# A two-layer hybrid attention trunk: the next pair's attention values projected beside a pair's first head, and head outputs read out of PSUM behind their products

## The chip, the cores and the metric

The kernel runs on one core of a Trainium2 chip. The metric is the time of one execution in microseconds on the device, the median of three runs; a profile of one further execution gives the trace that is read here. PE is the matrix engine (its weight loads are listed apart as PEld), DVE the vector engine, ACT the scalar engine, POOL the GpSimd engine, SP the engine that issues most transfers.

## The reference

A trunk of two layers over 256 latent tokens `x` and 256 context tokens `ctx`, 1024 wide. In each layer a token mixer with three branches is followed by a feed-forward network with a convolution over three tokens:

- differential attention, 8 heads: two softmaxes per head, `w = p0 - lam * p1`, the head's output `w @ v`, then a root-mean-square norm over the 128 features of the head with a learned gain and a factor `1 - lam_init`;
- a chunked gMLP;
- a bidirectional HGRN2 recurrence, 8 heads, whose output gets a root-mean-square norm with a gain (`hg_norm_g`) and a product with `silu(g)`.

```
y_att = rmsnorm(o_att, att_subln_g) * (1 - lam_init)
y_hg  = rmsnorm(o_f + flip(o_b), hg_norm_g) * silu(g)
```

In the first layer the queries are all 512 tokens (`NQ = 512`), in the second only the 256 latent ones (`NQ = 256`); keys, values and the recurrence run over all 512 in both. The result is the latent stream.

## The kernel before

All activations stand transposed (features on the partitions) in the tile `X`, as a high and a low part in float32r; each product of two float32 numbers is made of three matmuls (`mm3`, lines 120 to 123). `load_w` (line 115) fetches a weight block of 512 KB in two parts of 128x1024: a transfer on SP (line 110), a cast to the high part on ACT (line 111), and the subtraction that gives the low part on DVE (line 112).

The stage of the change is the loop over the eight heads, lines 936 to 1003, once per layer. For each head `project` makes what the head needs: the gates, queries and output gates of the recurrence (`hg_proj`, line 367: 4 feature-major projections, `fm_steps`), queries and keys of the attention with their rotation (`att_proj`, line 568: 2 feature-major projections), and for every even head the values of a pair of heads, for the recurrence (`w_hi`) at the start and for the attention (`w_av`) at the end (`v_proj`, line 398, by `tm_steps`). `v_proj` gives one tile of 128 x 4 x 256 for both heads of a pair, copied out of PSUM by ACT (line 405); three such tiles exist.

A head's own work is two generators, the side work: `hg_head` (line 408; 13 steps between its yields) and `att_head` (line 588; 11 steps in the first layer, 7 in the second). The order in which PE gets its instructions is the order in which the program is written (`manual_schedule` for PE, line 1208); for the other engines a scheduler of the compiler orders what is ready. `weave` (line 821) writes PE's order: it runs `project(h + 1)` step by step and puts the side steps of head `h` between them, evenly over 0.92 of the steps that `units(h + 1)` announces: 12 for an odd head to be projected and 20 for an even one in the first layer, 9 and 17 in the second. So the side work of an even head lies beside the projection of an odd one, and the other way round. Head 7 is woven with `tail_proj` instead.

```
todo = sorted((((i + 1) / (c + 1) * n * rate, k) for k, c in enumerate(counts) for i in range(c)))
```

At the end of a head `rms_square` (line 314) squares the output `o` out of its PSUM bank on ACT (line 316), casts the squares (line 192, ACT) and subtracts (line 193, DVE); a step of `weave` later `rms_scale` (line 323) sums them over the partitions with two matmuls into another bank (line 321) and makes the reciprocal root on ACT (lines 327, 328). Then DVE reads `o` a second time: line 550 in `hg_head`, followed by the product with the gate of line 551, and line 644 in `att_head`. `put` stores the result to DRAM through SP.

PSUM has two pools of four banks: `pm` for the projections, `ps` for the heads (scores, levels, turned weights, `o`, column sums).

Of the kernel before, what the change touches and what calls it, by code (L numbers as in the profile page):

```python
# [13 lines left out]
AF = mybir.ActivationFunctionType  # L14
# [3 lines left out]
P = 128  # L18
# [3 lines left out]
HEADS = 8  # L22
# [25 lines left out]
def trunk(ctx: ExitStack, tc: tile.TileContext, A, out):  # L48
    nc = tc.nc
    sub, mul, add, amin, amax = ALU.subtract, ALU.mult, ALU.add, ALU.min, ALU.max  # L50
# [9 lines left out]
    @contextmanager  # L60
    def pool(name, side="left", **tags):
        with tc.tile_pool(name=name, bufs=1, side=side, reuse_waits="tile") as p:
            def get(tag, shape, dt=F32):
                return p.tile(shape, dt, tag=tag, name=tag, bufs=tags[tag])
            yield get
# [34 lines left out]
    def pk(l, n):  # L100
        a, b = PK[n]
        return pack[l][:, a:b]
# [211 lines left out]
    def rms_square(get, o, n):  # L314
        sq = get("sq", [P, 512])
        nc.scalar.activation(out=sq[:, :n], in_=o, func=AF.Square)
        return sq, split(get("sqs", [P, 2, n], F32R), sq[:, :n])
# [80 lines left out]
    def v_proj(get, src, X, out, name, w=None):  # L398
        if w is None:
            w = load_w(src)  # L400
        v = get("v", [P, 4, 256])
        for tt in range(2):
            ps = PB([P, 2, 256])
            yield from tm_steps(w, X, (2 * tt, 2 * tt + 1), ps)
            nc.scalar.copy(out=v[:, 2 * tt:2 * tt + 2, :], in_=ps)
        out[name] = v

    def hg_head(get, l, h, z, k, q, gg, v, put, lbv, C0, NQ):
# [3 lines left out]
        if l > 0:  # L412
            s = get("E", [P, 2, NT])
            nc.scalar.activation(out=s, in_=z, func=AF.Exp)
            for d in range(2):
                nc.vector.tensor_scalar(out=s[:, d, :], in0=s[:, d, :], scalar1=lbv[:, 1, d, h:h + 1], scalar2=2.0 ** -60,
                                        op0=mul, op1=amax)
# [13 lines left out]
        sc = get("sc", [P, NS, 2, T])  # L431
# [108 lines left out]
        for s in range(NS):  # L540
# [3 lines left out]
            if s == 0:  # L544
                for d in range(2):
                    nc.tensor.matmul(o[:, c], lhsT=st[:, d, :], rhs=V[:, d, 0:T], start=False, stop=(d == 1))  # L546
        sq = rms_square(get, o, NQ)
        yield
        r = rms_scale(sq, NQ)
        nc.vector.scalar_tensor_tensor(out=r[:, :NQ], in0=o, scalar=pk(l, "hgn"), in1=r[:, :NQ], op0=mul, op1=mul)  # L550
        nc.vector.tensor_tensor(out=r[:, :NQ], in0=r[:, :NQ], in1=gg, op=mul)
        put(r[:, :NQ])

# [34 lines left out]
    def att_head(get, l, qk, v, put, av, NQ):  # L588
        sc = 64 ** -0.5
        o = None  # L590
# [39 lines left out]
        for i in range(n + 2):  # L630
# [7 lines left out]
            if 1 <= i <= n:  # L638
                ws[i - 1] = turn(*ps.pop(i - 1))
                yield  # L640
        sq = rms_square(get, o, NQ)
        yield
        r = rms_scale(sq, NQ)
        nc.vector.scalar_tensor_tensor(out=r[:, :NQ], in0=o, scalar=av[:, 1:2], in1=r[:, :NQ], op0=mul, op1=mul)
        put(r[:, :NQ])
        yield

# [288 lines left out]
    for l in range(DEPTH):  # L936
# [5 lines left out]
        def putter(b, h):  # L942
            return lambda t: nc.sync.dma_start(out=ysp[b, h], in_=t)
# [20 lines left out]
        whi = load_w(A["w_hi"][l, 0])  # L964
        pre = nc.scalar.preload_act_table_set("natural_log_exp_and_others")
        tc.keep_in_program_order(pre)
        with pool("heads", lk=2, qg=1, qk=1, v=3, w=2, sq=2, sqs=2 if l else 1, wt=2, sc=1, E=6 if l else 4, K=2, p=2) as get, ExitStack() as even, \
                tc.issue_after(pre.ins):
            gete = even.enter_context(pool("even", lk=2, qg=1, qk=1, t=3, sh=2))
            gets = [lambda tag, *a: (gete if tag in ("lk", "qg", "qk", "t", "sh") else get)(tag, *a),  # L970
                    lambda tag, *a: (gete if tag in ("t", "sh") else get)(tag, *a)]

            def project(h, out, pss=None):
                if pss is not None:
                    yield from hg_proj(gets[h % 2], l, h, Xh, NQ, out, pss)
                if h % 2 == 0:
                    yield from v_proj(get, A["w_hi"][l, h // 2], Xh, out, "vh", whi if h == 0 else None)
                if pss is None:
                    yield from hg_proj(gets[h % 2], l, h, Xh, NQ, out)
                yield from att_proj(gets[h % 2], l, h, Xh, rope, NQ, out)  # L980
                if h % 2 == 0:
                    yield from v_proj(get, A["w_av"][l, h // 2], Xh, out, "va")

            def units(h):
                return (12 if l == 0 else 9) + (8 if h % 2 == 0 else 0)

            d = {}
            for _ in project(0, d, first):
                pass
            for h in range(HEADS):  # L990
                j = slice((h % 2) * P, (h % 2 + 1) * P)
                m = [hg_head(get, l, h, d["ls"], d["k"], d["qg"][:, 0, :], d["qg"][:, 1, :], d["vh"][:, :, j], putter(1, h),
                             lbv, (reset, masks), NQ),
                     att_head(get, l, d["qk"], d["va"][:, :, j], putter(0, h), attv[l], NQ)]
                if h + 1 < HEADS:
                    main, n = project(h + 1, d), units(h + 1)
                else:
                    even.close()
                    getv = rvt.enter_context(pool("vt", side="right", vt=ns))
                    vt = [getv("vt", [P, D]) for _ in range(ns)]  # L1000
                    pus = []
                    main, n = tail_proj(l, Xh, vt, ns, NQ, pus), 8 * ns // 2 + ns
                weave(main, n, m, (13, 2 * ns + 3), 0.92 if h + 1 < HEADS else (0.7, 0.85)[l])
# [208 lines left out]
```

## Time and profile before

| what | value |
|---|---|
| median of 3 runs | 2232.55 us (2230.82 to 2233.64) |
| the profiled execution | 2240.42 us |
| its span, first to last instruction | 2238.6 us |
| mean granted clock of PE | 0.981 of full speed |
| instructions | 32836 |
| moved by DMA | 293.21 MB |

The profile is of one execution. Busy times of PE have modelled ends: two matmuls that follow each other overlap in it, so the distance of their starts is what one takes. A wait is put down to the engine and line that came last before it. Line numbers are those of the kernel before.

### The profile page before, as it was taken

The numbers are of one execution on the slowest core, as the hardware profiler recorded it, in microseconds if no ns is written. First come the engines' busy times: TensorE is split into PE (matmuls) and PEld (weight loads), VectorE is DVE, ScalarE is ACT, GpSimd is POOL, SyncE is SP. The second block draws the span as 40 slices with busy tenths as digits, with TensorE's granted clock in tenths as the row PEclk, the third lists the DMA queues.
The fourth block names the chain that finished last, engine by engine and source line by source line (L and its number), as shares of the span: only waits on it lengthen the run. The fifth ranks groups of instructions, "written<-read, shape, count | busy, mean of one in ns | idle before, by whom it ended". The sixth has DMA issues, their size and how long they took to land. (4 is left out here: it accounts for less than half of the span.)

```text
span 2238.6 us, 32836 instructions
## 1 busy us (share of the span) xinstructions
PE 2136.9 (95%) x12448; PEld 1860.9 (83%) x12448; DVE 1713.4 (77%) x2869; ACT 1155.8 (52%) x1920; POOL 315.7 (14%) x272
## 2 busy tenths in 40 slices
PE   8999999999999998989999998999999989997998
PEld 7888788887888886878887877988888879997997
DVE  6799888989767884358776766898899976567786
ACT  3766665656543223245342334666666655455664
POOL 3332132322200000011000002222221210001000
PEclk9999999999999999999999999999999999998999
DMA  7212212212255754344555653322222336654554
GB/s 283 94 67 73 70 66 76 73 65 66 62 174 193 235 161 112 94 159 136 166 187 182 198 148 105 104 91 90 81 90 86 97 99 218 195 183 142 186 194 138
DMA packets 93488, 293.21 MB, mean 131 GB/s; under 512 B 16017, under 2 KB 20753, under 8 KB 93073
## 3 DMA queue, kind: packets, MB, share of 16 engines
q1 hardware_dynamic: 93042, 290.59, 40.1%
q8 instruction: 98, 1.61, 0.3%
q14 instruction: 60, 0.49, 0.1%
q10 hardware_dynamic: 288, 0.52, 0.1%
HBM read 282.66 MB, written 8.41 MB: 130 GB/s over the span
## 5 line engine op out<-in xcount | busy, mean ns | idle before, releaser
L121 PE MATMUL pm<-X,wh 128*128 128x512 f32 (+1 forms) x2032 | 716.1, 352 | 11.0 <-DVE X L255 6.5
L122 PE MATMUL pm<-X,wh 128*128 128x512 f32 (+1 forms) x2032 | 699.0, 344 | 0.0
L123 PE MATMUL pm<-X,wl 128*128 128x512 f32 (+1 forms) x2032 | 698.8, 344 | 0.0
L112 DVE TENSOR_TENSOR wl<-wr,wh 128x1024 fp32r<-128x1024 f32 (+1 forms) x402 | 496.8, 1242 | 203.5 <-ACT wh L111 198.9
L111 ACT CAST wh<-wr 128x1024 fp32r<-128x1024 f32 x408 | 422.0, 1039 | 310.7 <-PE pm L122 172.2
L121 PEld LDWEIGHTS pm<-X,wh 128*128 128x128 f32 x2032 | 386.8, 190 | 61.2 <-DVE X L255 7.9
L123 PEld LDWEIGHTS pm<-X,wl 128*128 128x128 f32 x2032 | 387.1, 190 | 47.3
L122 PEld LDWEIGHTS pm<-X,wh 128*128 128x128 f32 x2032 | 386.5, 190 | 42.1
L225 DVE SCALAR_TENSOR_TENSOR wj<-wa,scr 128x1024 f32<-128x1024 f32 x128 | 156.4, 1222 | 63.4 <-DMA wa<-in_ada_row 60.4
L447 POOL TENSOR_TENSOR K<-qg,E 128x512 f32<-128x512 f32 (+1 forms) x96 | 132.3, 1380 | 461.9 <-PE ps L507 304.3
L121 PE MATMUL pm<-wl,X 128*128 128x256 f32 (+1 forms) x608 | 188.0, 309 | 0.0
L122 PE MATMUL pm<-wh,X 128*128 128x256 f32 (+1 forms) x608 | 183.7, 302 | 0.0
L123 PE MATMUL pm<-wh,X 128*128 128x256 f32 (+1 forms) x608 | 183.7, 302 | 0.0
L202 POOL TENSOR_TENSOR s<-s,mhalf 128x1 f32<-128x1 f32 x26 | 14.3, 550 | 1078.4 <-DVE s L199 1052.7
L121 PE MATMUL pm<-ys,wh 128*128 128x512 f32 (+1 forms) x384 | 129.9, 338 | 10.6 <-ACT wh L111 7.4
L441 DVE TENSOR_TENSOR E<-lk 128x512 f32<-128x512 f32 (+1 forms) x192 | 124.4, 681 | 9.5 <-PE ps L546 8.1
L123 PE MATMUL pm<-ys,wl 128*128 128x512 f32 (+1 forms) x384 | 129.5, 337 | 0.0
L122 PE MATMUL pm<-ys,wh 128*128 128x512 f32 (+1 forms) x384 | 129.5, 337 | 0.0
L121 PEld LDWEIGHTS pm<-wl,X 128*128 128x128 f32 x608 | 117.7, 194 | 6.5 <-issue 2.2
L122 PEld LDWEIGHTS pm<-wh,X 128*128 128x128 f32 x608 | 117.8, 194 | 4.0
L123 PEld LDWEIGHTS pm<-wh,X 128*128 128x128 f32 x608 | 117.4, 193 | 4.2
L442 ACT ACTIVATE E<-E 128x1024 f32<-128x1024 f32 (+1 forms) x96 | 80.9, 846 | 59.9 <-DVE E L441 58.9
(250 smaller groups left out, 3541.3 us busy)
## 6 DMA issues: line engine op xcount, KB each, us to landing
wr<-in_w_up SPq DMA_DIRECT2D x88, 512.0 KB, 4.4
wa<-in_ada_row SPq DMA_DIRECT2D x80, 512.0 KB, 4.1
wr<-in_w_gate SPq DMA_DIRECT2D x48, 512.0 KB, 4.0
wr<-in_w_dn SPq DMA_DIRECT2D x40, 512.0 KB, 4.1
wr<-in_w_hqg SPq DMA_DIRECT2D x32, 512.0 KB, 3.6
wr<-in_w_hff SPq DMA_DIRECT2D x32, 512.0 KB, 3.6
wr<-in_w_aqk SPq DMA_DIRECT2D x32, 512.0 KB, 3.6
wr<-in_w_hi SPq DMA_DIRECT2D x16, 512.0 KB, 4.0
```

The costliest lines, as they stand in the source:

```text
L111: nc.scalar.copy(out=hi, in_=raw)
L112: eng.tensor_tensor(out=lo, in0=raw, in1=hi.bitcast(F32), op=sub)
L121: nc.tensor.matmul(ps, lhsT=lh, rhs=rl, start=first, stop=False)
L122: nc.tensor.matmul(ps, lhsT=lh, rhs=rh, start=False, stop=False)
L123: nc.tensor.matmul(ps, lhsT=ll, rhs=rh, start=False, stop=last)
L202: nc.gpsimd.tensor_tensor(out=r, in0=r, in1=mhalf, op=ALU.pow)
L225: nc.vector.scalar_tensor_tensor(out=junk, in0=raw, scalar=1.0, in1=scr[:, v, :], op0=mul, op1=mul, accum_out=mod[l][:, m, v:v + 1])
L441: nc.vector.tensor_tensor(out=dst, in0=ref if first else src, in1=src if first else ref, op=sub)
L442: nc.scalar.activation(out=E, in_=E, func=AF.Exp)
L447: nc.gpsimd.tensor_tensor(out=mkap(KQ[:], dims, NQ), in0=mkap(q, dims), in1=mkap(E[:], [[2 * b, np_], [b - NQ, 2], [1, b]], NQ), op=mul)
```

## The change

`v_proj` now gives a list of two tiles of 128 x 4 x 128, one per head of a pair, out of six such tiles, and copies each half out of PSUM by itself. The attention values of the first pair are projected with head 0 as before; those of pair `c` (1 to 3) at the end of `project` of the odd head 2c - 1, which is woven with the side work of the even head 2c - 2. The recurrence's values stay at the start of the even head. `units` says 16 for heads 1 to 6 in the first layer (13 in the second) and 12 (9) for head 7.

In `hg_head` DVE multiplies `o`, its gain and the gate into the gate's tile `gg` right behind `rms_square`, before the yield; behind `rms_scale` one product is left. In `att_head` ACT copies `o` with its gain into a new tile `u` of the tag `wt` at the same place, and DVE's operation behind `rms_scale` multiplies two tiles in SBUF.

```diff
--- before.py
+++ after.py
@@ -398,11 +398,12 @@
     def v_proj(get, src, X, out, name, w=None):
         if w is None:
             w = load_w(src)
-        v = get("v", [P, 4, 256])
+        v = [get("v", [P, 4, P]) for _ in range(2)]
         for tt in range(2):
             ps = PB([P, 2, 256])
             yield from tm_steps(w, X, (2 * tt, 2 * tt + 1), ps)
-            nc.scalar.copy(out=v[:, 2 * tt:2 * tt + 2, :], in_=ps)
+            for i in range(2):
+                nc.scalar.copy(out=v[i][:, 2 * tt:2 * tt + 2, :], in_=ps[:, :, i * P:(i + 1) * P])
         out[name] = v
 
     def hg_head(get, l, h, z, k, q, gg, v, put, lbv, C0, NQ):
@@ -545,9 +546,9 @@
                 for d in range(2):
                     nc.tensor.matmul(o[:, c], lhsT=st[:, d, :], rhs=V[:, d, 0:T], start=False, stop=(d == 1))
         sq = rms_square(get, o, NQ)
+        nc.vector.scalar_tensor_tensor(out=gg, in0=o, scalar=pk(l, "hgn"), in1=gg, op0=mul, op1=mul)
         yield
         r = rms_scale(sq, NQ)
-        nc.vector.scalar_tensor_tensor(out=r[:, :NQ], in0=o, scalar=pk(l, "hgn"), in1=r[:, :NQ], op0=mul, op1=mul)
         nc.vector.tensor_tensor(out=r[:, :NQ], in0=r[:, :NQ], in1=gg, op=mul)
         put(r[:, :NQ])
 
@@ -639,9 +640,11 @@
                 ws[i - 1] = turn(*ps.pop(i - 1))
                 yield
         sq = rms_square(get, o, NQ)
+        u = get("wt", [P, NQ])
+        nc.scalar.activation(out=u, in_=o, func=AF.Copy, scale=av[:, 1:2])
         yield
         r = rms_scale(sq, NQ)
-        nc.vector.scalar_tensor_tensor(out=r[:, :NQ], in0=o, scalar=av[:, 1:2], in1=r[:, :NQ], op0=mul, op1=mul)
+        nc.vector.tensor_tensor(out=r[:, :NQ], in0=r[:, :NQ], in1=u, op=mul)
         put(r[:, :NQ])
         yield
 
@@ -964,34 +967,36 @@
         whi = load_w(A["w_hi"][l, 0])
         pre = nc.scalar.preload_act_table_set("natural_log_exp_and_others")
         tc.keep_in_program_order(pre)
-        with pool("heads", lk=2, qg=1, qk=1, v=3, w=2, sq=2, sqs=2 if l else 1, wt=2, sc=1, E=6 if l else 4, K=2, p=2) as get, ExitStack() as even, \
+        with pool("heads", lk=2, qg=1, qk=1, v=6, w=2, sq=2, sqs=2 if l else 1, wt=2, sc=1, E=6 if l else 4, K=2, p=2) as get, ExitStack() as even, \
                 tc.issue_after(pre.ins):
             gete = even.enter_context(pool("even", lk=2, qg=1, qk=1, t=3, sh=2))
             gets = [lambda tag, *a: (gete if tag in ("lk", "qg", "qk", "t", "sh") else get)(tag, *a),
                     lambda tag, *a: (gete if tag in ("t", "sh") else get)(tag, *a)]
 
             def project(h, out, pss=None):
+
                 if pss is not None:
                     yield from hg_proj(gets[h % 2], l, h, Xh, NQ, out, pss)
                 if h % 2 == 0:
-                    yield from v_proj(get, A["w_hi"][l, h // 2], Xh, out, "vh", whi if h == 0 else None)
+                    yield from v_proj(get, A["w_hi"][l, h // 2], Xh, out, ("vh", h // 2), whi if h == 0 else None)
                 if pss is None:
                     yield from hg_proj(gets[h % 2], l, h, Xh, NQ, out)
                 yield from att_proj(gets[h % 2], l, h, Xh, rope, NQ, out)
-                if h % 2 == 0:
-                    yield from v_proj(get, A["w_av"][l, h // 2], Xh, out, "va")
+                c = 0 if h == 0 else (h + 1) // 2 if h % 2 and h < HEADS - 1 else None
+                if c is not None:
+                    yield from v_proj(get, A["w_av"][l, c], Xh, out, ("va", c))
 
             def units(h):
-                return (12 if l == 0 else 9) + (8 if h % 2 == 0 else 0)
+                return (12 if l == 0 else 9) + (4 if h < HEADS - 1 else 0)
 
             d = {}
             for _ in project(0, d, first):
                 pass
             for h in range(HEADS):
-                j = slice((h % 2) * P, (h % 2 + 1) * P)
-                m = [hg_head(get, l, h, d["ls"], d["k"], d["qg"][:, 0, :], d["qg"][:, 1, :], d["vh"][:, :, j], putter(1, h),
+                vh, va = d["vh", h // 2][h % 2], d["va", h // 2][h % 2]
+                m = [hg_head(get, l, h, d["ls"], d["k"], d["qg"][:, 0, :], d["qg"][:, 1, :], vh, putter(1, h),
                              lbv, (reset, masks), NQ),
-                     att_head(get, l, d["qk"], d["va"][:, :, j], putter(0, h), attv[l], NQ)]
+                     att_head(get, l, d["qk"], va, putter(0, h), attv[l], NQ)]
                 if h + 1 < HEADS:
                     main, n = project(h + 1, d), units(h + 1)
                 else:
```

## Rows read from the trace of the kernel before

**Rows 1.** The page, part 1: busy time, share of the span, instructions.

```profile
PE 2136.9 (95%) x12448; PEld 1860.9 (83%) x12448; DVE 1713.4 (77%) x2869; ACT 1155.8 (52%) x1920; POOL 315.7 (14%) x272
```

**Rows 2.** Waits of PE, 64 to 640 us: waiter, releaser, total us, times, longest.

```profile
PE ps L321 <- DVE sqs L193: 6.6, 6, 1.8
PE ps L626 <- DVE sc L465: 4.6, 3, 1.5
```

**Rows 3.** Waits of PE, 1415 to 1850 us.

```profile
PE ps L321 <- DVE sqs L193: 10.3, 7, 2.7
PE ps L619 <- DVE p L613: 3.2, 1, 3.2
```

**Rows 4.** Busy time by stretch, layer 0: units beside head 1, head 2, the pair.

```profile
core 0: us, PE busy (x) PEld busy (x) DVE busy (x) ACT busy (x) POOL busy (x), PEclk, DMA share, GB/s
...
171.26:217.95 46.69, 46.35 (x259) 39.29 (x258) 44.58 (x77) 28.06 (x50) 13.96 (x9) 1.00 0.20 68
...
232.60:293.25 60.65, 55.32 (x294) 45.25 (x292) 57.01 (x98) 38.37 (x68) 17.37 (x10) 0.97 0.20 70
156.34:293.25 136.91, 131.24 (x778) 112.54 (x776) 118.38 (x204) 83.31 (x146) 38.45 (x26) 0.99 0.21 70
```

**Rows 5.** The same, layer 1: beside head 3, head 4, the pair, the slow clock.

```profile
1606.67:1638.12 31.45, 31.45 (x202) 28.16 (x201) 26.53 (x47) 19.43 (x37) 4.54 (x6) 1.00 0.31 101
...
1653.58:1695.10 41.52, 38.00 (x239) 32.27 (x238) 39.01 (x77) 27.46 (x54) 8.56 (x9) 0.99 0.29 96
1590.14:1695.10 104.96, 100.55 (x666) 89.71 (x666) 93.70 (x187) 67.46 (x130) 22.37 (x24) 0.97 0.26 86
1589.60:1595.30 5.70, 5.70 (x27) 5.70 (x28) 5.70 (x15) 3.24 (x7) 1.41 (x2) 0.50 0.15 42
```

**Rows 6.** PE in order of time: start us, us, line, [idle before <- releaser].

```profile
1586.26 0.40 PE L122 MATMUL pm<-X,wh 128*128 128x512 f32 x1
1586.49 0.39 PE L123 MATMUL pm<-X,wl 128*128 128x512 f32 x1
1589.57 0.77 PE L321 MATMUL ps<-sqs,onesr 128*128 128x256 f32 x2 [2.69 <-DVE sqs L193]
...
1595.79 0.28 PE L121 MATMUL pm<-wl,X 128*128 128x256 f32 x1
1595.91 0.28 PE L122 MATMUL pm<-wh,X 128*128 128x256 f32 x1
```

**Rows 7.** DVE by line, pair of layer 0: xcount | busy us, mean ns.

```profile
L112 DVE TENSOR_TENSOR wl<-wr,wh 128x1024 fp32r<-128x1024 f32 x16 | 20.9, 1309 | 4.5 <-ACT wh L111 4.5
...
L361 DVE SCALAR_TENSOR_TENSOR t<-pm,t 128x512 f32<-128x512 f32 x4 | 2.7, 683 | 0.4 <-ACT t L356 0.4
...
L374 DVE SCALAR_TENSOR_TENSOR lk<-pm,t 128x512 f32<-128x512 f32 x4 | 2.7, 678 | 0.0
...
L577 DVE STREAM_SHUFFLE sh<-pm 128x256 f32<-128x256 f32 x4 | 1.8, 445 | 0.0
...
L550 DVE SCALAR_TENSOR_TENSOR sq<-ps,pack,sq 128x512 f32<-128x512 f32 x2 | 1.5, 744 | 0.0
...
L551 DVE TENSOR_TENSOR sq<-sq,qg 128x512 f32<-128x512 f32 x2 | 1.4, 690 | 0.0
```

**Rows 8.** DVE by line, pair of layer 1.

```profile
L361 DVE SCALAR_TENSOR_TENSOR t<-pm,t 128x256 f32<-128x256 f32 x4 | 1.7, 416 | 0.1
...
L550 DVE SCALAR_TENSOR_TENSOR sq<-ps,pack,sq 128x256 f32<-128x256 f32 x2 | 1.0, 476 | 0.0
```

**Rows 9.** ACT by line, pair of layer 0.

```profile
L316 ACT ACTIVATE sq<-ps 128x512 f32<-128x512 f32 x4 | 2.4, 596 | 3.2 <-PE ps L543 3.2
L405 ACT COPY v<-pm 128x512 f32<-128x512 f32 x4 | 2.3, 580 | 2.7 <-PE pm L123 2.7
...
L621 ACT COPY wt<-ps 128x256 f32<-128x256 f32 x4 | 1.4, 359 | 0.1
```

## The prediction

> **What bounds the kernel now.** I read the page's busy shares first: PE is busy 95% of the span and DVE 77% [rows 1]. The stages with `project` and the heads (64 to 640 us and 1415 to 1850 us) are where the diff acts, so next I asked for PE's waits there. The longest are the column sums of line 321, which wait for DVE's split of line 193: 6.6 us in layer 0 and 10.3 us in layer 1 [rows 2, 3]. PE runs in the written order, so whatever DVE delivers late stops the projections queued behind it too.
>
> Then I cut one pair of heads at the boundaries of the projections. Call a unit the stretch between two yields of `project`. A feature-major unit is 12 matmuls of 512 columns, 0.23 us apart, 2.76 us; a value unit is 24 of 256 columns, 0.12 us apart, 2.88 us [rows 6]. While an odd head's side work runs, PE has 20 units to weave it into in layer 0 (17 in layer 1); for an even head it has 12 (9). In layer 0 the 12 feature-major units take 46.69 us beside an odd head and 60.65 us beside an even one, with DVE busy in 57.01 us of the latter [rows 4]; in layer 1 the 9 units take 31.45 and 41.52 us, DVE 39.01 us of the latter [rows 5].
>
> How much of that is loss? `weave` spreads a head's side steps over 0.92 of the units. In layer 0 the 46.69 us hold 12 of 18.4 such units, 65% of a head's side work: (46.69 - 33.1) / 0.65 = 20.8 us of side matmuls a head. Beside an even head all of it falls in: 33.1 + 20.8 = 53.9 us without loss, so **6.7 us are lost**; over the whole pair 24 x 2.76 + 8 x 2.88 + 41.6 = 130.8 of 136.91 us. In layer 1: (31.45 - 24.8) / 0.575 = 11.6 us; 36.4 without loss, 5.1 us lost there; the pair 95.9 of 104.96, **9.1 us lost**. Part of it is the clock: after the 2.69 us wait at 1589.57 the granted clock was 0.50 of 2.4 GHz for the next 5.70 us [rows 5, 6], about 2.9 us of work.
>
> **Why DVE is late.** Its work per pair is 118.38 us in layer 0 and 93.70 us in layer 1 [rows 4, 5]. The projections' share: 16 weight splits of line 112, 20.9 us, of which four belong to the values (5.2 us); lines 374 and 375, 2.7 us each; 361 and 363, 2.7 us each (1.7 in layer 1); four rotation lines like 577, 6.8 us together (6.1) [rows 7, 8]. Without the values that is 16.7 us a head in layer 0 and 15.4 us in layer 1, which leaves 39.9 and 28.8 us of side work a head. So beside an even head DVE has 16.7 + 39.9 = 56.6 us of work against PE's 53.9 (2.7 short), and 44.2 against 36.4 in layer 1 (7.8 short).
>
> **Part 1, the moved projection.** Three times a layer, four value units go from beside an odd head to beside the even head before it: 16 units (13) for each. The last even head keeps 12 (9). No matmul is added; the weights of `w_av` (two 512 KB issues on SP, two casts on ACT, two splits on DVE per load) move with them, from half a pair later; the DMA share of 0.20 to 0.29 leaves room, and the stores of `put` that SP issues between the loads keep their number. Six half-width tiles hold what three full ones held: beside an even head four are live and two are free, so the new copies find a slot without a wait.
>
> Side steps now spread over 14.7 units (12.0). Layer 0, beside an even head, in the 12 feature-major units: 81.5% of the side work, PE 33.1 + 17.0 = 50.1 us, DVE 16.7 + 32.5 + 2.6 for the value weights = 51.8: 1.7 short. Beside an odd head 73%: PE 48.3, DVE 45.8, 2.5 to spare. Against 2.7 short with a loss of 6.7, a loss of about 2.7 stays: **4 us gained per pair**, bounds 0 and 6.7. Layer 1: even 33.5 against 39.6 (6.1 short), odd 32.6 against 34.7 (2.1 short). These two runs now follow each other, because the value units of both sides have come together: 8.2 short in one run where it was 7.8. So the shortage in layer 1 doesn't shrink. What goes is the end of the even head: its last products and column sums, where the 2.69 us wait and the slow clock stand, fall among value units, which ask DVE for little. I take **2 us gained per pair**, nearer the low end; bounds 9.1 gained and 3 lost (the 2.1 short of the odd head added whole, with 0.9 of clock). Sum of part 1: 3 x 4 + 3 x 2 = 18 us, from 9 lost to 47 gained.
>
> **Narrower evictions.** 32 copies of 128x512 at 580 ns become 64 of 128x256, like those of line 621 at 359 ns: +4.4 us on ACT [rows 9]. ACT is busy 83.31 of 136.91 us and 67.46 of 104.96 us per pair [rows 4, 5]; the four `pm` banks cover a copy 0.14 us later in all. Zero; without the cover 4.4 us.
>
> **Part 2, reading `o` at once.** No wait on PE in these stages is put down to lines 550 or 644, so an earlier free bank gives nothing that I can see; upper bound for a gain 1 us, the longest waits for a bank being in the middle of a head. In the attention head ACT gets one more pass over the bank, priced as line 316's 596 ns in layer 0, and the last DVE operation changes from a PSUM read like line 550's to line 551's form, 744 to 690 ns [rows 7, 9]: 16 heads, under 1 us of DVE saved. The new tile takes one of two `wt` slots when the last turned weights have been used; the next head needs one only after its second score step, so nobody waits. In the HGRN head the 744 ns (476 ns in layer 1 [rows 8]) stand on DVE between the square and the split that PE waits for, if the scheduler puts them first. What is queued behind them is the split of line 193, and behind that the column sums. From 0 to 8 x 0.74 + 8 x 0.48 = 9.8 us lost; I take 1 us, since the operation behind the sums gets shorter by the same and only late sums count.
>
> The Trainium skill's page "ScalarE: Activation LUTs", section "Rules for kernel authors", sends a multiplication to VectorE and not to ScalarE. The trace speaks otherwise here: ACT passes over the same bank in 596 ns [rows 9], DVE in 744 [rows 7], and ACT has the idle time; by the page's rule the attention edit would cost, by the rows it costs nothing.
>
> **Sum.** -18 + 1 = -17 us. The profiled execution took 2240.4 us (its span 2238.6); 2223 by this. It lay 7.9 us over the median of the runs, 2232.55, so for a run I forecast **2216 us**.
>
> **The rivals.** *Balance clears the loss* (chance 0.16): the carry into a run is small, DVE's idle moments vanish, and both layers run near PE's own time: 3 x 6.5 + 3 x 9 = 47 us, 2186 us. For it: DVE's 118.38 and 93.70 us per pair fit into 130.8 and 95.9. Against it: 93.70 of 95.9 leaves 2% for an engine that idles 6% even where it is late.
>
> *The backlog only moves* (0.18): the joined runs (24 units of layer 0, 18 of layer 1, with no value unit between) take back what the even heads gain: 0 to 5 us, 2230 us. For it: the 8.2 against 7.8 in layer 1. Against it: layer 0 has 2.5 to spare in front of its shortage.
>
> *The early read delays the column sums* (0.11), the slower one: in every HGRN head DVE takes `o` first, after ACT's square of 596 ns, and the split comes after it. Price: 9.8 us for the operation, and 8 x 0.6 + 8 x 0.4 = 8.0 us for standing at the head of DVE's queue until the square is done: 18 us. It decides once DVE's order has the read in front of the split and the shortage leaves no slack to hide it; with a gain of part 1 of at most 8 the time is 2243 us. The Trainium skill, page "PSUM — Partial Sum Buffer", section "Terms", has ACT's and DVE's reads of one bank exclude each other, so the read would follow the square; no row here shows such a pair. For the rival: the largest wait of both stages is on just this split [rows 2, 3]. Against it: a DVE that is late reaches the read when the square is long done.
>
> *The change doesn't reach what it names*: the moved units leave the last even head as it was (12 units, 9), so that loss stays in every case above.
>
> **How the numbers follow.** Forecast 0.55, with 2200 to 2228 its own range; the others 0.16, 0.18, 0.11. About 0.2% (4.5 us) is what a measurement of this kernel can tell from no change. Faster: 0.55 + 0.16 + a quarter of the moved backlog = 0.75; same 0.14; slower 0.11. The range runs from 2196 us, half of the balanced case, to 2236 us, the moved backlog with its whole spread.
>
> **What would show it.** Cut at the value units: in layer 0 the feature-major units beside even heads should take about 53 us, not 60.65, beside odd heads 48 to 50; in layer 1 about 38 and 34. The waits of line 321 should fall in sum, and the slow-clock stretch at the start of value units should be gone. If 321's waits grow in the HGRN heads and line 193 stands behind the new read, the slower rival is right. A span of a pair under 132 and 97 us would make me wrong on the other side.

## The result, and the profile after

The changed kernel takes 2270.78 us (median of 4 runs, 2266.35 to 2273.9) against 2233.1 us: the ratio is 1.0169, 95% interval 1.015 to 1.0188. The forecast was 2216 us, faster; the measurement is outside the range, and of the other sign.

First the page, part 1, of the kernel after, to be held against [rows 1]:

```profile
PE 2143.2 (95%) x12448; PEld 1865.2 (82%) x12448; DVE 1716.7 (76%) x2869; ACT 1166.8 (51%) x1968; POOL 296.3 (13%) x272
```

The busy times hardly differ: ACT has the 48 instructions of the narrower copies and the new passes (+11.0 us), DVE as many as before. The time went into waiting. Next the waits of PE after, first over 64 to 640 us, then over 1415 to 1860 us (total us, times, longest), as in [rows 2, 3]:

```profile
PE ps L321 <- DVE sqs L193: 17.0, 8, 3.9
PE ps L508 <- DVE sc L466: 7.3, 6, 1.6
PE ps L528 <- DVE E L520: 4.6, 3, 1.6
...
PE ps L321 <- DVE sqs L193: 10.4, 6, 4.0
PE ps L603 <- POOL qk L586: 4.7, 3, 1.6
```

The wait that the change was to shorten, line 321 on the split, went from 6.6 to 17.0 us in layer 0 and stayed at 10 in layer 1. L528 (L527 of the kernel before) is new in the list, and so is L508's wait for `sc`; its line waited before too (L507), for `K`, 2.7 us.

The windows after (us, busy time of each engine, PEclk, DMA share, GB/s): the two stages from the first value unit to the end of the last; then one pair of each layer, cut as in [rows 4, 5] into the feature-major units beside the odd head, those beside the even head, and the eight value units that now stand together; last, what follows the longest wait of that pair in layer 0.

```profile
64.07:648.38 584.31, 547.52 (x3200) 467.73 (x3200) 486.94 (x833) 349.11 (x620) 137.41 (x96) 0.99 0.21 68
1434.86:1869.05 434.19, 406.58 (x2656) 360.26 (x2655) 376.94 (x747) 278.90 (x549) 91.39 (x96) 0.98 0.27 88
185.36:239.40 54.04, 49.80 (x270) 41.72 (x269) 49.79 (x83) 34.17 (x60) 15.42 (x10) 1.00 0.19 64
239.40:290.30 50.90, 49.35 (x269) 40.37 (x268) 47.51 (x87) 31.84 (x59) 12.91 (x10) 1.00 0.20 68
290.30:326.50 36.20, 32.95 (x246) 30.86 (x244) 22.80 (x37) 19.13 (x36) 5.07 (x5) 0.95 0.22 73
1531.83:1566.19 34.36, 34.09 (x218) 30.27 (x217) 26.55 (x48) 21.81 (x43) 4.22 (x5) 1.00 0.31 97
1566.19:1603.60 37.41, 34.31 (x216) 29.35 (x215) 36.34 (x80) 28.44 (x55) 13.29 (x12) 1.00 0.27 89
1603.60:1638.91 35.31, 31.10 (x239) 29.27 (x237) 30.09 (x61) 18.52 (x41) 6.80 (x7) 0.95 0.20 66
296.67:300.20 3.53, 3.53 (x17) 3.34 (x18) 2.33 (x4) 2.30 (x4) 1.72 (x2) 0.60 0.27 102
```

And the two stages in the kernel before, cut in the same way:

```profile
64.28:626.90 562.62, 544.27 (x3199) 466.67 (x3199) 481.22 (x832) 343.19 (x596) 157.98 (x96) 0.99 0.21 71
1416.24:1840.94 424.70, 403.63 (x2657) 357.32 (x2655) 378.31 (x747) 274.56 (x525) 90.25 (x96) 0.98 0.28 90
```

So the profiled executions differ by 21.7 us in layer 0 and 9.5 us in layer 1, which is the whole difference of their spans, 2267.8 to 2238.6, within 2 us. (The profiled run of before lay above its median, so the medians differ by more, 37.7 us.) Of the pairs:

| us | beside odd | beside even | value units | pair |
|---|---|---|---|---|
| layer 0 before | 46.69 | 60.65 | 29.57 | 136.91 |
| layer 0 after | 54.04 | 50.90 | 36.20 | 141.14 |
| layer 1 before | 31.45 | 41.52 | 32.00 | 104.96 |
| layer 1 after | 34.36 | 37.41 | 35.31 | 107.08 |

The even heads got the relief that was forecast. The odd heads of layer 0 and the value units gave back more. So did the last even head of each layer, which is in none of these pairs and which the change left its 12 (9) units: its feature-major units, before and after in layer 0,

```profile
505.04:562.96 57.92, 53.53 (x294) 44.08 (x293) 55.56 (x98) 37.71 (x68) 18.34 (x8) 1.00 0.24 73
520.42:584.24 63.82, 54.27 (x294) 44.34 (x293) 59.23 (x102) 39.25 (x71) 18.58 (x13) 0.99 0.22 66
```

take 5.9 us more, and in layer 1 4.9 us more (46.20 for 41.31): 10.8 of the 31.2 us that the two stages lost. The rows of PE in order of time show where (start, us, in brackets the wait): four beside an odd head of layer 0, then the column sums that stand among the value units, of layer 0 and of layer 1, and at the end two waits of the last even head of layer 0, at its first scores and its last column sums.

```profile
206.94 1.13 PE L508 MATMUL ps<-K 128*128 128x128 f32 x8 [1.56 <-DVE sc L466]
209.62 0.44 PE L620 MATMUL ps<-ident,p 128*128 128x128 f32 x2 [0.66 <-ACT p L609]
222.73 0.66 PE L528 MATMUL ps<-ident,E 128*128 128x128 f32 x4 [1.54 <-DVE E L520]
226.63 0.73 PE L321 MATMUL ps<-sqs,onesr 128*128 128x512 f32 x2 [0.49 <-DVE sqs L193]
...
296.67 1.19 PE L321 MATMUL ps<-sqs,onesr 128*128 128x512 f32 x2 [3.25 <-DVE sqs L193]
...
1622.51 0.50 PE L321 MATMUL ps<-sqs,onesr 128*128 128x256 f32 x2 [3.76 <-DVE sqs L193]
...
525.01 0.98 PE L603 MATMUL ps<-qk 64*128 64x512 f32 x6 [1.67 <-POOL qk L586]
...
583.25 1.19 PE L321 MATMUL ps<-sqs,onesr 128*128 128x512 f32 x2 [3.92 <-DVE sqs L193]
```

Beside the odd head of [rows 4] the only wait was one of 0.34 us.

### The profile page after: what moved, and what is told of

The parts are those of the page before. It is cut to its first block, busy times and chain, and to the rows that moved or that the text cites. A ratio compares the mean times of both kernels' runs of the same rounds, so it can differ in the third digit from the quotient of the medians.

```text
span 2267.8 us, 32881 instructions
## 1 busy us (share of the span) xinstructions
PE 2143.2 (95%) x12448; PEld 1865.2 (82%) x12448; DVE 1716.7 (76%) x2869; ACT 1166.8 (51%) x1968; POOL 296.3 (13%) x272
## 5 line engine op out<-in xcount | busy, mean ns | idle before, releaser
L112 DVE TENSOR_TENSOR wl<-wr,wh 128x1024 fp32r<-128x1024 f32 (+1 forms) x402 | 501.9, 1254 | 209.0 <-ACT wh L111 203.0
L448 POOL TENSOR_TENSOR K<-qg,E 128x512 f32<-128x512 f32 (+1 forms) x96 | 121.9, 1271 | 471.5 <-PE ps L508 290.5
L442 DVE TENSOR_TENSOR E<-lk 128x512 f32<-128x512 f32 (+1 forms) x192 | 114.0, 625 | 12.9 <-PE ps L547 9.0
```

The source lines that it names most:

```text
L112: eng.tensor_tensor(out=lo, in0=raw, in1=hi.bitcast(F32), op=sub)
L442: nc.vector.tensor_tensor(out=dst, in0=ref if first else src, in1=src if first else ref, op=sub)
L448: nc.gpsimd.tensor_tensor(out=mkap(KQ[:], dims, NQ), in0=mkap(q, dims), in1=mkap(E[:], [[2 * b, np_], [b - NQ, 2], [1, b]], NQ), op=mul)
```

## The experiments

Line numbers move by a few lines from kernel to kernel; the tiles tell which operation a row is. "Loss" is a pair's length less what it takes without loss by the prediction's working, 130.8 us in layer 0 and 95.9 in layer 1.

### The parts alone

**The move alone** (part 1 with the narrower copies; both heads read `o` as before), as a diff to the kernel after:

```diff
-        nc.vector.scalar_tensor_tensor(out=gg, in0=o, scalar=pk(l, "hgn"), in1=gg, op0=mul, op1=mul)
...
+        nc.vector.scalar_tensor_tensor(out=r[:, :NQ], in0=o, scalar=pk(l, "hgn"), in1=r[:, :NQ], op0=mul, op1=mul)
...
-        u = get("wt", [P, NQ])
-        nc.scalar.activation(out=u, in_=o, func=AF.Copy, scale=av[:, 1:2])
...
+        nc.vector.scalar_tensor_tensor(out=r[:, :NQ], in0=o, scalar=av[:, 1:2], in1=r[:, :NQ], op0=mul, op1=mul)
```

> The moved projection and the half-width value tiles, with o read as before. Theory M (the move itself costs: the feature-major units of two heads now follow each other, and a head's first scores stand right behind the projection of its queries and keys): nearly all of the 38 us stays, 2260 to 2275 us, and PE's waits on line 585 (queries and keys) are 1.6 us at each even head of layer 1. Theory R (the early reads cost, by standing between the squares and their split): the move alone gains what was forecast, 2215 to 2230 us.

**The reads alone** (the values as before; of the change only the edits to `hg_head` and `att_head`; the lines added to the kernel before):

```diff
+        nc.vector.scalar_tensor_tensor(out=gg, in0=o, scalar=pk(l, "hgn"), in1=gg, op0=mul, op1=mul)
...
+        u = get("wt", [P, NQ])
+        nc.scalar.activation(out=u, in_=o, func=AF.Copy, scale=av[:, 1:2])
...
```

> The early reads of o alone, with the values projected as before. Theory M: within 5 us of the kernel before, 2228 to 2238 us. Theory R: slower, 2245 to 2270 us, with PE's wait for the split of line 193 in the HGRN heads above the 17.0 us of before and the read standing before that split on DVE. If both parts are slower by less than the whole, the two costs add.

**The narrower copies alone** (two tiles of 128 x 4 x 128 out of six; projected where they were; against the kernel before):

```diff
-        v = get("v", [P, 4, 256])
+        v = [get("v", [P, 4, P]) for _ in range(2)]
...
-            nc.scalar.copy(out=v[:, 2 * tt:2 * tt + 2, :], in_=ps)
+            for i in range(2):
+                nc.scalar.copy(out=v[i][:, 2 * tt:2 * tt + 2, :], in_=ps[:, :, i * P:(i + 1) * P])
```

> Half-width value tiles and 64 narrow evictions in place of 32 wide ones, nothing moved, o read as before. Theories M and R alike: no change, 2228 to 2238 us. A third theory, that the narrow evictions or the six tiles change ACT's order enough to cost: slower by 5 us or more.

Measured: the move 2256.78 us, 1.0131 (1.0106 to 1.0156); the reads 2245.33, 1.008 (1.0056 to 1.0104); the copies 2231.0, 1.0006 (0.9988 to 1.0024). So both parts cost time, 28.1 and 16.7 us against the runs of before beside them, and the copies nothing. The costs overlap: their sum, 44.8 us, is more than the 37.7 us of both together; both lengthen the waits of the column sums (in 64 to 600 us from 6.6 to 10.7 us by the move and to 21.4 by the reads, 17.0 with both). The move's kernel has the table's pattern already: 54.07 us beside the odd head and 50.91 beside the even one. Its last even heads take 60.29 and 44.23 us, half of what the change adds to them.

### Why the move costs

**The values at the start of the odd head's projection**, so that no two runs of feature-major units join (diff to the kernel after; reads as before):

```diff
+                if h % 2 and h < HEADS - 1:
+                    yield from v_proj(get, A["w_av"][l, (h + 1) // 2], Xh, out, ("va", (h + 1) // 2))
...
-                c = 0 if h == 0 else (h + 1) // 2 if h % 2 and h < HEADS - 1 else None
-                if c is not None:
-                    yield from v_proj(get, A["w_av"][l, c], Xh, out, ("va", c))
+                if h == 0:
+                    yield from v_proj(get, A["w_av"][l, 0], Xh, out, ("va", 0))
```

> As the first of these, but the next pair's attention values come at the start of an odd head's projection, so value units and feature-major units alternate evenly as before (4 value units, then 12 or 9 others, in every head). Theory M: the joined runs are the cost, so this is as fast as the kernel before or faster, 2205 to 2235 us. Theory R: like the run with the values at the end, 2215 to 2230 us.

Measured: 2263.83 us, 1.0163 (1.0139 to 1.0187), no better than the move alone. One of its waits beside an even head:

```profile
288.86 0.66 PE L528 MATMUL ps<-ident,E 128*128 128x128 f32 x4 [1.53 <-DVE E L520]
```

Joined runs aren't what makes these waits. But now every head of layer 0 but the last two, odd or even, has four value units ahead of its 12 feature-major ones, and every one has the four waits of the odd head above, to within 0.05 us. They don't go with the head or its neighbours. That made the next theory, the pace: `weave` puts 13 HGRN steps into 14 equal parts, so an odd head's were 18.4 / 14 = 1.31 units apart and after the move 14.7 / 14 = 1.05, and between some steps stands a chain over ACT, DVE and POOL that needs longer than that.

The kernel after itself shows that the pace doesn't choose the waits alone. Its even heads have the same steps at the same unit boundaries as its odd ones, over the same 14.7 units; only the four value units lie behind the feature-major ones and not ahead. One of their rows:

```profile
276.09 1.13 PE L508 MATMUL ps<-K 128*128 128x128 f32 x8 [0.88 <-DVE sc L466]
```

In their feature-major units the waits are 0.32, 0.88 and 0.24 us, L528 has none, and the column sums wait later, the 3.25 us among the value units: 4.7 us a head where an odd head waits 4.25, but at other steps.

**Only the pace**: the kernel before, nothing moved, an odd head's steps spread as densely as the move spreads them:

```diff
-                weave(main, n, m, (13, 2 * ns + 3), 0.92 if h + 1 < HEADS else (0.7, 0.85)[l])
+                weave(main, n, m, (13, 2 * ns + 3), (0.92 * units(1) / units(2) * ((16 / 12), (13 / 9))[l] if h % 2 else 0.92) if h + 1 < HEADS else (0.7, 0.85)[l])
```

> The kernel before with nothing moved; only the rate of the weave is cut for odd heads, from 0.92 to 0.736 in layer 0 and 0.704 in layer 1, so that their side steps come as close together as in the changed kernel (13 steps in 14.7 and 12.0 units instead of 18.4 and 15.6). Theory P (pace: the loss of a head jumps up once its steps stand about one unit apart, so two heads at the middle pace lose more than one at a fast and one at a slow pace): 10 to 20 us slower, 2240 to 2250 us, with new waits beside odd heads at the lines that wait beside them in the run with the move alone (508, 620, 528, 321). Theory J (joined runs or the place of the move itself): within 4 us of the kernel before.

Measured: 2258.35 us, 1.0122 (1.0079 to 1.0165); the profiled run, 2249.23, was the lowest of a wide four (to 2267.15). PE beside the first odd head:

```profile
194.44 1.13 PE L507 MATMUL ps<-K 128*128 128x128 f32 x8 [1.60 <-DVE sc L465]
197.12 0.44 PE L619 MATMUL ps<-ident,p 128*128 128x128 f32 x2 [0.66 <-ACT p L608]
210.24 0.66 PE L527 MATMUL ps<-ident,E 128*128 128x128 f32 x4 [1.54 <-DVE E L519]
214.13 0.72 PE L321 MATMUL ps<-sqs,onesr 128*128 128x512 f32 x2 [0.48 <-DVE sqs L193]
```

and its window beside the next odd head (beside the first and the third it took 53.62 us):

```profile
312.92:367.00 54.08, 49.61 (x268) 41.47 (x267) 48.52 (x80) 32.89 (x58) 15.57 (x10) 1.00 0.18 64
```

The four waits are there with no value moved, and the odd head's stretch is 53.6 to 54.1 us, as after. Nothing was added to DVE here, so the rate of the weave alone brings these waits. The rate sets two things, how far apart the steps stand and beside which unit each falls; this run doesn't part them.

**The odd heads' pace given back to the move**: the moved kernel with reads as before, in which the pair's own attention values are projected a second time at the old place, into a tile that nobody uses (ACT copies 32 of every 128 columns), so that odd heads have their 20 (17) units again:

```diff
+                elif h % 2 == 0:
+                    yield from v_proj(get, A["w_av"][l, h // 2], Xh, {}, "again", None, 32)
...
-                return (12 if l == 0 else 9) + (4 if h < HEADS - 1 else 0)
+                return (12 if l == 0 else 9) + ((8 if h % 2 == 0 else 4) if h < HEADS - 1 else 0)
```

> The move alone, and besides the attention values of the current pair projected a second time at the place where they were before (two reads of a corner of each result, nothing uses them), so that odd heads have 20 and 17 units beside them again and even heads 16 and 13. It adds 4 units, 11.4 us of PE, to each of six pairs: 68 us. Pace theory (an odd head loses when its steps come as close as about one unit): the waits beside odd heads go, about 4 us a pair in layer 0, so its pairs take 146 to 149 us and the whole 2295 to 2315 us. Place theory (the loss comes from the value units' new place, at the end of the odd projection): pairs of 151 to 153 us, the whole 2320 to 2335 us.

Measured: 2295.04 us, 1.0285 (1.0253 to 1.0317), with 3 x 2 x 11.4 = 68 us of PE's work added. Its windows: beside the odd head, beside the even head, the pair of layer 0, that of layer 1:

```profile
183.91:230.58 46.67, 46.34 (x259) 39.30 (x258) 44.56 (x77) 28.14 (x50) 13.82 (x9) 1.00 0.20 68
245.23:296.09 50.86, 49.31 (x269) 40.37 (x268) 47.43 (x85) 31.70 (x59) 10.82 (x8) 1.00 0.19 68
183.91:331.47 147.56, 143.03 (x876) 124.76 (x874) 121.91 (x207) 86.79 (x157) 31.79 (x24) 0.99 0.21 72
1544.19:1656.84 112.65, 110.36 (x762) 100.46 (x760) 97.31 (x190) 70.65 (x142) 20.93 (x25) 0.98 0.26 90
```

The odd head is back at 46.67 us, before's 46.69; the even head keeps its 50.9. Less the 11.4 us added to a pair, the loss is 5.4 us in layer 0 (move alone 9.8) and 5.4 us in layer 1 (move alone 12.4). What stays in layer 0 stands among the eight value units, which take 35.4 us. The added units also give DVE more time per pair; here the two can't be told apart, in the paced kernel they can, and there the rate alone makes the stretch of layer 0.

### Is it the order on ACT and DVE?

PE's order is written out, those of ACT and DVE are the scheduler's, and edits of a line or two changed them in many places. The order theory: the column sums are late since the next head's level work (differences on DVE, exponentials on ACT) stands ahead of their split. It is tried by holding that work behind the cast and the split, in the moved kernel, in that with the reads, and in the kernel before:

```diff
+        ahead_of[:] = [nc.scalar.copy(out=parts[:, 0, :], in_=sq[:, :n]),
+                       nc.vector.tensor_tensor(out=parts[:, 1, :], in0=sq[:, :n], in1=parts[:, 0, :].bitcast(F32), op=sub)]
...
+                for i in ahead_of:
+                    behind.enter_context(tc.issue_after(i.ins))
+                return level_(b)
```

> The move alone, with the next head's level work (subtractions on DVE, exponentials on ACT) held behind the split of the last squares in each engine's queue. Theory O (order: the split that the column sums wait for stands in the queues behind work for the next head, put there by the compiler's schedule): PE's waits on line 193 fall from 24.8 us to under 10, and the time from 2257 to 2235 to 2245 us. Theory P: waits on 193 fall a little, the time stays above 2250.

> The early reads alone, with the same hold. Theory O: the 17 us that the reads cost come from the changed order alone, so the time returns to 2225 to 2233 us and the waits on line 193 to 17 us or less. If the reads themselves cost, by standing on DVE ahead of the split: 2238 to 2248 us still.

> The kernel before with the same hold and nothing else. Theory O: of its 17 us of waits on line 193 most go, 2215 to 2228 us. If the hold makes DVE and ACT stand idle for the squares instead, so that the next head's levels come late: 2230 us or more, with the waits moved to lines 507 and 465.

Measured: 2262.01 us, 1.0134 (1.0101 to 1.0167); 2253.13, 1.0106 (1.0073 to 1.0138); 2252.03, 1.0098 (1.0067 to 1.0129). The moved kernel is no faster by it, that with the reads not either, and the kernel before loses 20 us. The column sums' waits went in all three (in the moved kernel from 24.8 to 4.4 us), and others came. The longest wait of PE, in sum, in the moved kernel with the hold (L614 scores), the whole span:

```profile
PE ps L614 <- ACT p L620: 16.1, 10, 1.9
```

and in the kernel before with it (L518 the turned keys), 64 to 600 us:

```profile
PE ps L518 <- DVE K L456: 10.9, 4, 3.1
```

What is put behind the split is late for the next head. The order decides which wait is seen; with this hold the time doesn't fall. A finer order was not tried on the moved kernel.

### Which of the reads costs

**The HGRN head's read alone, and the attention head's pass alone**, each the kernel before with that half of the reads' diff:

> Of the early reads only the HGRN head's on DVE. If this read is the cost (it stands on DVE ahead of the split and behind the square): nearly all of the 17 us, 2243 to 2250 us, with the waits on line 193 in layer 0 near 21 us. If the attention head's pass on ACT is the cost: 2228 to 2236 us. If it is the schedule of both engines that any such edit turns over: between, 2234 to 2243.

> Of the early reads only the attention head's on ACT. The counterpart of the run before: 2228 to 2236 us if the HGRN read is the cost, 2243 to 2250 us if this pass is, between if either turns the order over.

Measured: the read on DVE 2224.77 us, 0.9982 (0.9965 to 1.0000); the pass on ACT 2237.91, 1.0052 (1.0031 to 1.0073). The first is the best version found, at most a little faster than before; the second costs some 9 us. The column sums wait 7.9 us in 64 to 600 us with the first, 13.8 with the second and 21.4 with both.

The longest of those, in the kernel with both reads: ACT, then DVE, then POOL and PE, in order of time.

```profile
293.33 0.60 ACT L316 ACTIVATE sq<-ps 128x512 f32<-128x512 f32 x1 [0.71 <-PE ps L543]
297.47 1.06 ACT L442 ACTIVATE E<-E 128x1024 f32<-128x1024 f32 x1 [3.54 <-DVE E L441]
298.44 0.60 ACT L192 CAST sqs<-sq 128x512 fp32r<-128x512 f32 x1
...
294.46 2.31 DVE L112 TENSOR_TENSOR wl<-wr,wh 128x1024 fp32r<-128x1024 f32 x1
296.70 1.28 DVE L441 TENSOR_TENSOR E<-lk 128x512 f32<-128x512 f32 x2
297.90 0.74 DVE L548 SCALAR_TENSOR_TENSOR qg<-ps,pack,qg 128x512 f32<-128x512 f32 x1
...
299.16 0.68 DVE L193 TENSOR_TENSOR sqs<-sq,sqs 128x512 fp32r<-128x512 f32 x1
...
294.02 1.68 POOL L460 TENSOR_TENSOR E<-E,qg 128x512 f32<-128x512 f32 x1 [0.78 <-DVE E L458]
...
299.99 0.77 PE L321 MATMUL ps<-sqs,onesr 128*128 128x512 f32 x1 [3.92 <-DVE sqs L193]
```

ACT had the square done at 293.93 us, but an exponential of the next head stood between it and the cast and waited 3.54 us for DVE; the early read of line 548 is 0.74 of the 5.2 us from the square to the split, and a weight split that took 2.31 us, beside POOL, stands in them too. In the kernel before ACT cast straight behind the square:

```profile
289.06 0.60 ACT L316 ACTIVATE sq<-ps 128x512 f32<-128x512 f32 x1 [1.24 <-PE ps L543]
289.69 0.62 ACT L192 CAST sqs<-sq 128x512 fp32r<-128x512 f32 x1
```

**Both reads, ACT's exponentials held behind the cast** (the hold above, with only the cast as what goes first), **the attention pass queued behind the cast**, and **both reads queued behind cast and split**:

```diff
+                for i in ahead_of[:1]:
+                    behind.enter_context(tc.issue_after(i.ins))
...
+        with tc.issue_after(cut[0].ins):
+            nc.scalar.activation(out=u, in_=o, func=AF.Copy, scale=av[:, 1:2])
...
+        with tc.issue_after(cut[1].ins):
+            nc.vector.scalar_tensor_tensor(out=gg, in0=o, scalar=pk(l, "hgn"), in1=gg, op0=mul, op1=mul)
```

> Both early reads, with only ACT's exponentials of the next head's levels held behind the cast of the squares; DVE's order is left free. If the cast that stands behind such an exponential on ACT is what makes the column sums late: the waits on line 193 fall below 10 us and the time to 2225 to 2238 us. If DVE's own order (the read and the subtractions ahead of the split) does it: the waits on 193 stay above 15 us and the time above 2240.

> The attention head's early pass on ACT alone, but queued behind the cast of the squares instead of between the square and the cast. If its place in front of the cast is what it costs: back to 2224 to 2232 us, with the waits on line 193 in layer 0 from 13.8 us to about 8. If the pass costs wherever it stands: 2235 to 2245 us.

> Both early reads, ACT's behind the cast and DVE's behind the subtraction, nothing moved. If order is all that the reads cost: 2222 to 2232 us and waits on line 193 in layer 0 under 10 us instead of 21.4. If the compiler's order of the rest turns over whenever the reads are there: 2238 to 2250 us, with the exponentials of the next head's levels still between square and cast.

Measured: 2238.13 us, 1.0044 (1.0023 to 1.0065); 2237.86, 1.0035 (1.0024 to 1.0047); 2252.0, 1.0095 (1.008 to 1.011). The cast first takes about 7 us off both reads, from 1.008 to 1.0044 (the two intervals just overlap), just past the upper end of what was expected; the waits of PE that then lead in 64 to 600 us are the scores (L613), and the column sums (L326) are nearly gone:

```profile
PE ps L613 <- POOL qk L596: 7.0, 4, 1.9
...
PE ps L326 <- DVE sqs L321: 3.1, 8, 0.6
```

The place of the reads themselves isn't the cost: behind cast and split they cost as much as in front of them, with 22.2 us of waits on the split in layer 0, and the pass alone costs much the same behind the cast (1.0035) as in front of it (1.0052).

### A slower weave for all

**The kernel before with its steps over all the units**, rate 1.0 for 0.92 (the same line as the pace's diff):

> The kernel before with the rate of the weave at 1.0 in place of 0.92 for all heads but the last: steps stand 9% further apart beside odd and even heads alike. By the pace theory the even heads' loss shrinks while the odd ones keep none: 2215 to 2230 us, if the sums at the very end of a head don't then wait against the next head's first scores; if they do, 2233 to 2245 us.

Measured: 2272.0 us, 1.0192 (1.0166 to 1.0218). Beside an odd head and then at the end of an even one, layer 0, PE in order of time:

```profile
224.88 0.33 PE L527 MATMUL ps<-ident,E 128*128 128x128 f32 x1 [1.66 <-DVE E L520]
...
295.84 1.03 PE L543 MATMUL ps<-sc,v 128*128 128x256 f32 x4
303.68 1.22 PE L321 MATMUL ps<-sqs,onesr 128*128 128x512 f32 x2 [6.82 <-DVE sqs L193]
```

With no unit left between the last products and the column sums, PE stands 6.82 us for the chain square, cast, split. That is how long this chain, with what stands in its queues, keeps PE where nothing covers it, and the four such waits are 27.3 us in layer 0 and 18.4 in layer 1, where the kernel before waits 6.6 and 10.3 for the split: 29 of the 43 us that the slower weave lost. So the last step wants units behind it. The rest speaks against distance alone: beside the odd heads of layer 0, whose steps stand further apart than before (20 / 14 = 1.43 units), line 527 waits 1.66 us, as in the dense weave, and their feature-major units take 47.9 us for 46.69. Beside which unit a step falls counts too.

## Why the prediction was wrong

**The even heads: right.** Forecast about 53 and 38 us beside an even head, measured 50.90 and 37.41; beside odd heads of layer 1 about 34, measured 34.36. The balance of DVE's and PE's work per stretch told these.

**Odd heads of layer 0: the step that failed.** "2.5 to spare" gave 48 to 50 us; every stretch of 12 feature-major units behind four value units, woven over 14.7 units, took 53.6 to 54.2 us, after, in the moved kernel, with the values at the start, and in the paced kernel. The prediction took DVE's loss for a shortage of its total. DVE was busy in 49.79 of the 54.04 us; 4.25 us are four waits of PE for single operations of DVE and ACT. That a chain between two steps is there longer than the steps are apart is the reading that fits; no such chain was timed link by link, and the even heads of the same kernel, with the same steps at the same pace, wait at other steps. Engines with time to spare in sum don't shorten such a wait. Three odd heads make some 12 of the 21.7 us that layer 0 lost. What is left over 48.3 us, 1.5 us, may be the error of an even share, since the steps are unequal; no run shows it.

**The end of the even head: the second step that failed.** "Fall among value units, which ask DVE for little" was to end the 2.69 us wait and the slow clock. The last products do fall there, and the column sums wait 3.25 and 3.76 us, with a granted clock of 0.60 over the next 3.53 us. The value units are 36.20 us where 23.0 + 0.455 x 20.8 = 32.5 would be without loss, in layer 1 35.31 where 29.8 would be: 3.7 and 5.5 us a pair. These units follow the projection of queries and keys directly, and DVE was not free. In layer 0 the cast was done at 292.71 us, and until the split DVE did the rotation of the queries and keys, a weight split and one level subtraction:

```profile
293.32 1.66 DVE L112 TENSOR_TENSOR wl<-wr,wh 128x1024 fp32r<-128x1024 f32 x1
...
295.85 0.68 DVE L193 TENSOR_TENSOR sqs<-sq,sqs 128x512 fp32r<-128x512 f32 x1
```

In layer 1 the last products were done at 1615.92 us and their square began on ACT at 1620.51, behind exponentials of the next head's levels that waited for DVE.

**The last even head: put at nothing.** "So that loss stays in every case above" took it for unchanged, since its units are; it lost 5.9 and 4.9 us, over a third of the whole. In layer 0 two waits make 5.6 us of it: 1.67 us of its first scores for POOL's rotated queries and keys (the four moved value units used to stand between the two), and 3.92 us of the last column sums. With the move alone the first is 1.48 and the second 0.20 us. In layer 1 its scores wait 1.57 us in the same way and its turned weights 2.17 us, against none and 0.74 us before, but its column sums wait no longer; what makes the rest of the 4.9 us stays open.

**The early reads: mis-sized.** 1 us was taken, out of 0 to 9.8; measured alone 16.7 us. The slower rival named place and size (18 us for the reads), and waits on the split did grow, from 6.6 to 21.4 us in layer 0. Its mechanism fell, though: the HGRN read on DVE alone costs nothing, and queued behind the split the reads cost the same. The pass on ACT, which "by the rows costs nothing", costs 0.5% alone. I held its duration against ACT's idle time; the rows show another order on ACT once the instruction is there, and an exponential ahead of the cast that passes DVE's delay on to PE. The Trainium skill's page "ScalarE: Activation LUTs", section "Rules for kernel authors", which sends a multiplication to VectorE, fared better than my reading: the read on DVE is the part that is free. Its reason, the time per element, isn't what these rows show, where ACT's pass is the shorter one; that attention's on DVE would be free too was not run.

**The rivals.** That the backlog only moves (2230 us) is nearest for the move, and too small, since the odd heads' pace isn't in it. The balance that clears the loss is refuted: the pairs are 141.14 and 107.08 us, not under 132 and 97. The Trainium skill's page "PSUM — Partial Sum Buffer", section "Terms", has ACT and DVE not read a bank at once. The kernel after shows such a pair, ACT's square and DVE's early read of the same `o`:

```profile
1620.51 0.37 ACT L316 ACTIVATE sq<-ps 128x256 f32<-128x256 f32 x1
...
1620.91 0.48 DVE L549 SCALAR_TENSOR_TENSOR qg<-ps,pack,qg 128x256 f32<-128x256 f32 x1 [1.03 <-ACT sq L316]
```

The read begins 0.03 us behind the square's end, after 1.03 us of waiting: this one pair agrees. Whether the program or the bank holds it is not told apart.

**What stays open.** Whether the odd heads lose by the distance of the steps or by the units that they fall beside: the paced kernel changes both, and the even heads of the kernel after and the slower weave show that distance alone doesn't choose the waits. Why both reads cost 0.8% where one is free and the other costs 0.5% is told only as far as this: the order of ACT differs, and putting the cast first takes 7 of the 17 us. In layer 1 the move's share of pace isn't settled: pacing alone lengthened that stage by only 4.0 us, while giving the odd heads their units back took 7.0 us off the loss of a pair. The paced kernel's median, 26 us above before, is more than its profiled run shows, in which layer 0 is 14.0 us longer and layer 1 4.0.

## What to carry to other kernels

Where side work is woven into a stream of other work, the length of the stream sets the distance of the steps: moving filler from one stretch to another thins one and packs the other, so ask of the packed one whether the longest chain between two steps still fits in, and beside which units the steps now fall, and not only whether each engine's sum does. Look at the stretch that keeps its length as well: here the last even head, whose neighbours moved, lost over a third of the whole. An instruction on an engine with idle time is free only if it doesn't come between others in a chain that someone waits for; where a scheduler orders that engine, try each such edit alone. A wait that goes by reordering is worth nothing until the time has fallen too.

## What was not expected of the hardware

A DVE operation took far longer beside POOL: the weight split L112 at 294.46 us above took 2.31 us, with POOL's L460 on until 295.70, against a mean of 1.309 us in [rows 7]. In the kernel before, 9 of the 72 splits between 64 and 640 us took 1.64 to 2.26 us, each of them beside a POOL operation for 0.56 us or more; the other 63 took under 1.3 us, 15 of them beside POOL as well. The Trainium skill's page "GPSIMD Engine Reference", section "1. Specifications", has POOL share its way to SBUF with DVE operations that take two inputs from there, as this one does; the rows agree, and they show which meetings cost. In all nine POOL's operation had begun first, and the split ended 1.08 to 1.09 us after it; in 12 of the 15 the split had begun first and took its usual time (the other three lie in POOL operations listed with 6.3 us). It was not tried by an edit. The second: a woven stretch repeats closely. The same four waits came to within 0.06 us each in four kernels, beside different heads.
